# A loop over leftover tokens moves in front of the last group of experts, and TensorE multiplies identities during the routing

## The chip, the cores and the metric

The kernel runs on one core of a Trainium2 chip. The time is the device time of one execution in microseconds (us), the median of several runs. TensorE (PE in the profile) multiplies; VectorE (DVE), ScalarE (ACT) and GpSimd (POOL) do elementwise work; SyncE (SP) issues most DMAs, in the order in which its program has them. Weight loads of TensorE are listed as PEld. Each engine runs its own program in order and waits for the others through semaphores.

## What is computed

One decoder layer on 512 tokens of width 1024, in float32. A state-space mixer and a convolution mixer are added to the residual stream h; then comes a mixture of experts; then a gate with per-layer embeddings p; then a norm. The change touches the mixture of experts and its surroundings:

```
u = rms_norm(h)
group  = argmax(u @ wg + bg)                    # 4 groups of 8 experts
expert = top 2 of the 8 logits in that group    # 1024 assignments, 32 experts
h += sum over the two: weight * (silu(u @ w_gate[e]) * (u @ w_up[e])) @ w_down[e]
h += (p @ w_ple_proj) * sigmoid(rms_norm(h) @ w_ple_gate)
out = rms_norm(h)
```

An expert's three matrices are 1024 x 512, 1024 x 512 and 512 x 1024 numbers, 6 MB together. All 32 experts are read, 192 MB.

## The kernel before

**Stages.** Up to about 530 us of the profile the mixers run. Then the routing picks two experts for each token (lines 1507 to 1592). The experts follow in seven groups (`GROUPS`, from the table `PLAN` in line 52), and last the gate stage, whose steps are the functions named `e_...`.

**Slots.** Each expert has a fixed number of slots for tokens, 32, 64 or 96, by its rank in popularity. A group is one or two "quads" of 128 slots, and a quad is filled by two or three experts. The last group is a single quad of three experts. For a group, `disp` gathers its tokens: four calls, each 16 multiplications of the normalised tokens (`u2h` in tile uh, `u2l` in tile ul) with one-hot matrices, and one copy by ScalarE into a tile cj. `gu_unit` multiplies cj with the gate and up matrices, in four units per quad; `d_unit` multiplies the hidden values with the down matrix, in two units per quad. A unit of a three-expert quad needs three pages of weights of 1 MB each. `combine` adds a group's output back to h (tile Z), in eight calls; each is four multiplications for a group of two quads and two for the last group, and an addition on VectorE. `back` prepares the matrix for it and is the last reader of a group's one-hot matrix.

**Order of the work.** `units` is the list of such units, and `step` runs one: it issues the weight loads for which there is room (`pump`, line 270), then the unit's multiplications, then the jobs hung on that unit. Tasks such as `disp` and `combine` have an earliest and a latest unit, and `after` (line 341) starts them between units where a running credit allows. Weight pages live in a tile w of 11 buffers, some of which hold other data for a time; a load waits until TensorE has read the page that it overwrites. `p_unit` (line 1327) multiplies the embeddings p with w_ple_proj; there are two, placed just ahead of the last group's units. `split_hi` and `split_lo` turn loaded float32 weights into a high and a low part, on ScalarE and VectorE.

**The loop.** Tokens beyond an expert's slots are handled in a hardware loop, `tc.For_i(0, n_ext)` in line 1704, whose count n_ext is computed on the chip. The loop loads an expert's weights in pieces of 512 KB (line 1772). Before it, `run(NC)` has run all units of all groups; after it the gate stage starts with transposes of h (`e_tr`). At the loop SP waits for every load that it has issued, and all engines wait for each other.

Of the kernel before, what the change touches and what calls it, by code (L numbers as in the profile page):

```python
# [52 lines left out]
GROUPS = []  # L53
# [83 lines left out]
def tile_hybrid(ctx: ExitStack, tc: tile.TileContext, x, p, chan, rowv, rows, cst, w_in, w_ssd, w_conf, w_o,  # L137
                rw, eg, eu, ed, w_pg, w_pp, out, dbg=None):
    nc = Core(tc.nc)
# [6 lines left out]
    def st(shape, dt, tag, bufs=1):  # L146
        return sb.tile(shape, dt, name=tag, tag=tag, bufs=bufs)

    def acc():
        return ps.tile([128, 512], F32, name="acc", tag="acc", bufs=6)  # L150
# [4 lines left out]
    def mm(o, a, b, start, stop):  # L155
        nc.tensor.matmul(o, a, b, start=start, stop=stop)
        if b.dtype == F32:
            nc.pe[0] += max(0.1, 3 * o.shape[-1] / 2370)
# [21 lines left out]
    identr = st([128, 128], F32R, "identr")  # L180
# [4 lines left out]
                            pattern=[[1, 128]], channel_multiplier=-1)  # L185
    negr = st([128, 128], F32R, "negr")
    nc.vector.tensor_copy(negr, negm)

    def junk():
        return st([128, D], BF, "k2", 4)  # L190
# [56 lines left out]
    units = []  # L247
# [8 lines left out]
    def unit(src, mms, cost=0.0, plain=False):  # L256
        srcs = [] if src is None else src if isinstance(src, list) else [src]
        units.append(dict(lds=[load(s, plain) for s in srcs], mms=mms, cost=cost, plain=plain))
        return len(units) - 1

    def job(n, f, *a):
        jobs[n].append((f, a))
# [4 lines left out]
    def task(early, late, cost, f, *a):  # L267
        tasks.append((early, late, cost, f, a))
# [86 lines left out]
    def step():  # L355
        n = state["n"]
        top = state["top"]
        if n < NB:
            while state["split"] <= min(max(n + 2, 2 * n - NB + BT["sp"]), top):
                split()  # L360
        else:
            while state["split"] <= min(top, n + BT["hi"]) and split_hi():
                split_lo()
        pump()
        u = units[n]
        if u["plain"]:
            ws = [ld["t"] for ld in u["lds"]]
            u["mms"](ws)
            free(2 * len(ws))
        elif u["mms"] is not None:  # L370
            u["mms"](u["wh"], u["wl"])
        after(u)

    def run(upto=None):
        while state["n"] < (len(units) if upto is None else upto):
            step()
# [517 lines left out]
    n = 0  # L894
# [147 lines left out]
    def p_mm(c, wh, wl):  # L1042
        pj["s"] = pt = acc()
        cs = slice(c * 128, (c + 1) * 128)
        for k in range(2):
            mm(pt, pj["h"][:, k, cs], wh[:, k, :], k == 0, False)
            mm(pt, pj["h"][:, k, cs], wl[:, k, :], False, False)
            mm(pt, pj["l"][:, k, cs], wh[:, k, :], False, k == 1)

    def p_out(n, c):  # L1050
        if c % 2 == 0:
            pj["o", n, c // 2] = page([128, 2, T], F32, "po")
        nc.scalar.activation(pj["o", n, c // 2][:, c % 2, :], pj.pop("s"), AF.Copy, scale=0.5)
# [43 lines left out]
    def rout_mm(c, n):  # L1097
        t = R.pop(("t", c, n))
        for k in range(4):
            mm(R["pl"][:, c * 36:(c + 1) * 36], t[:, k, :], R["rws"][:, 4 * n + k, :],  # L1100
               n == 0 and c == 0 and k == 0, n == 1 and c == NT - 1 and k == 3)
# [97 lines left out]
    def gu_unit(gi, q, i, kp):  # L1199
        quad = GROUPS[gi][q]  # L1200

        def mms(ws):
            if kp == 0:
                PG[gi, q, i] = acc()
            for kk in range(4):
                k = 4 * kp + kk
                strips(PG[gi, q, i], XT[gi, k // 2][:, k % 2, q * QS:(q + 1) * QS], [w[:, kk, :] for w in ws], quad,
                       k == 0, k == KD - 1)
        return unit([lambda b=m[0]: weights((eg, eu)[i], b)[:, 4 * kp:4 * kp + 4, :] for m in quad], mms, BT["mm"],
                    True)  # L1210

    def d_unit(gi, q, fp):
        quad = GROUPS[gi][q]

        def mms(ws):
            if fp == 0:
                PY[gi, q] = [acc2(), acc2()]
            for f in (2 * fp, 2 * fp + 1):
                for n in range(2):
                    strips(PY[gi, q][n], HT[gi, q][:, f, :], [w[:, f % 2, n * 512:(n + 1) * 512] for w in ws], quad,  # L1220
                           f == 0, f == 3)
        return unit([lambda b=m[0]: weights(ed, b)[:, 2 * fp:2 * fp + 2, :] for m in quad], mms, BT["mm"], True)
# [43 lines left out]
    def disp_mm(gi, kp, pt, a):  # L1266
        w = GW[gi]
        for kk in range(2):
            k = 2 * kp + kk
            for c in range(NT):  # L1270
                mm(pt[:, kk * w:(kk + 1) * w], R[("u2h", "u2l")[a]][:, c, k * 128:(k + 1) * 128],
                   G["oh", gi][:, c, :w], a == 0 and kk == 0 and c == 0, a == 1 and kk == 1 and c == NT - 1)

    def disp_out(gi, kp, pt):
        w = GW[gi]
        t = st([128, 2, w], F32, "cj", 9)
        nc.scalar.copy(t, pt[:, :2 * w].rearrange("p (k s) -> p k s", k=2))  # L1277
        XT[gi, kp] = t

    def disp(gi, kp):  # L1280
        pt = acc()
        for a in range(2):
            disp_mm(gi, kp, pt, a)
        disp_out(gi, kp, pt)
# [42 lines left out]
    def p_unit(n):  # L1327
        def mms(wh, wl):
            for c in range(NT):
                p_mm(c, wh, wl)  # L1330
                p_out(n, c)
        return unit(lambda: w_pp.rearrange("(k p) n -> p k n", p=128)[:, :, n * 512:(n + 1) * 512], mms, 5.5)
# [2 lines left out]
        fill_pe(state["n"], room)  # L1335

    combined = NB + 4
    for gi, g in enumerate(GROUPS):
        last = gi == len(GROUPS) - 1
        first = len(units)  # L1340
        if last:
            for n in range(2):
                p_unit(n)
            job(first - 6, free, -2)
            job(first - 5, p_load)
            job(first - 5, free, -2)
            for k in range(2):
                job(first - 3 + k, p_tr, k)
            job(first - 2, free, 2)
            job(first - 2, free, -8)  # L1350
        for q in range(len(g)):
            for kp in range(2):
                for i in range(2):
                    u = gu_unit(gi, q, i, kp)
            job(u - 1, hid_act, gi, q)
            job(u, hid_mul, gi, q)
            job(u, fill_now, BT["fill"][0])
            job(u, hid_tr, gi, q)
            job(u, fill_now, BT["fill"][1])
            if last:  # L1360
                job(u - 1, free, -2)
            for f in range(2):
                u = d_unit(gi, q, f)
            task(combined, u - 1, 1.4, back, gi, q)
            if last:
                job(u - 1, free, -2)
            for n in range(2):
                job(u, y_hi, gi, q, n)
                job(u, y_lo, gi, q, n)
        if last:  # L1370
            for n in range(2):
                for c in range(NT):
                    job(u, combine, gi, c, n)
            continue
        for n in range(2):
            for c in range(NT):
                task(u + 1, u + 5, 0.23 * 2 * len(g), combine, gi, c, n)
        combined = u + 5
        o = first + (BT["late"][0] if gi == 0 else BT["late"][1])
        for q in range(len(GROUPS[gi + 1])):  # L1380
            job(o, hot, gi + 1, q)
        for kp in range(4):
            task(o + 1, u, 0.115 * 16, disp, gi + 1, kp)
    for i in range(3):
        unit(None, None)
    NC = len(units)
# [121 lines left out]
    rout_tr(NT - 1, 1)  # L1508
    for c in (2, 3):
        rout_mm(c, 1)  # L1510
    if dbg == "h1":
        for c in range(NT):
            nc.sync.dma_start(out[c * 128:(c + 1) * 128, :], h[:, c, :])
        return
# [64 lines left out]
    for c in range(NT):  # L1579
        o = pp[:, c * NEXP:(c + 1) * NEXP]  # L1580
# [113 lines left out]
    for k in range(4):  # L1694
        disp_out(0, k, pts[k])
        if k % 2:
            step()
            step()
    run(NC)

    W32 = [128, NEXP]
    ext, ntot, icnt, eidf, pos, gat = (R[n] for n in ("ext", "ntot", "icnt", "eidf", "pos", "gat"))
# [1 line left out]
    with tc.For_i(0, n_ext):  # L1704
# [43 lines left out]
        for k in range(KD):  # L1748
            pt = acc()
# [33 lines left out]
        for w in (eg, eu):  # L1783
            o = acc()
# [9 lines left out]
        pt = acc()  # L1794
# [30 lines left out]
                nc.vector.tensor_add(hv, hv, po)  # L1825
        nc.vector.tensor_scalar(icnt, icnt, 1.0, None, op0=OP.add)
    banks.remove(bank)
    if dbg == "moe":
        for c in range(NT):
            nc.sync.dma_start(out[c * 128:(c + 1) * 128, :], h[:, c, :])  # L1830
        return
# [77 lines left out]
```

## Time and profile before

| | us |
|---|---|
| median of 3 runs (1109.29 to 1111.02) | 1109.32 |
| the profiled execution | 1109.12 |
| its span, first to last instruction | 1107.4 |
| TensorE busy in the span | 1017.9 (92%) |
| VectorE busy | 562.2 (51%) |
| ScalarE busy | 344.6 (31%) |
| mean share of the 16 DMA engines on SP's queue | 60.1% |

TensorE's share is high throughout, and a mean over the span says little, since the stages have different limits. From about 555 to 1034 us the DMA engines are full; before that and after it they are mostly idle. Rows of a timeline give start and duration in us, the engine, the operation, the tile written and the tiles read, the shape, and the count of instructions merged in the row. A float32 multiplication stands as two records, so 32 records of a unit are its 16 instructions. In brackets stands the idle time before and what ended it.

### The profile page before, as it was taken

How to read it: one execution, taken by the hardware profiler on the slowest of the kernel's cores; microseconds unless marked ns; L12 is line 12 of the kernel's file. 1: busy time of each engine (PE TensorE's matmuls, PEld its weight loads, DVE VectorE, ACT ScalarE, POOL GpSimd, SP SyncE). 2: the span in 40 equal slices, each digit the busy share in tenths (PEclk: the TensorE clock that was granted, in tenths of full speed). 3: DMA queues.
4: the chain of work that ended last, by engine and by line, in shares of the span. 5: the costliest groups of instructions: out<-in, count | busy, mean ns of one | idle time of the engine just before them, and what ended most of it. 6: DMA issues, size and time to landing. Idle time of an engine off the chain costs nothing. (4 is left out here: it accounts for less than half of the span.)

```text
span 1107.4 us, 15682 instructions
## 1 busy us (share of the span) xinstructions
PE 1017.9 (92%) x6262; PEld 675.5 (61%) x6262; DVE 562.2 (51%) x1004; ACT 344.6 (31%) x646; POOL 15.5 (1%) x32
## 2 busy tenths in 40 slices
PE   5999999999979989999799998988979989799876
PEld 5788889877868877788634543433525434344555
DVE  6689998897789955663621302203102012022564
ACT  5433446766442234433411110100100101030353
POOL 1000000000000000000000000000000000000020
PEclk9999999999999999999899999999999999999988
DMA  9323232202224323265199999999999999999401
GB/s 268 99 69 107 77 87 67 77 1 77 68 65 118 86 77 114 77 234 222 39 382 388 392 376 423 420 421 421 421 421 420 421 421 420 418 377 422 178 1 76
DMA packets 95660, 255.97 MB, mean 231 GB/s; under 512 B 4784, under 2 KB 62144, under 8 KB 71008
## 3 DMA queue, kind: packets, MB, share of 16 engines
q1 hardware_dynamic: 94896, 252.73, 60.1%
q0 software_dynamic: 688, 2.22, 0.7%
q8 instruction: 50, 0.82, 0.3%
q14 instruction: 26, 0.21, 0.1%
HBM read 252.83 MB, written 2.10 MB: 230 GB/s over the span
## 5 line engine op out<-in xcount | busy, mean ns | idle before, releaser
L120 PE MATMUL acc<-uh,w 128*128 128x512 f32 x704 | 231.0, 401 | 1.7 <-DVE w L120 1.6
L120 PE MATMUL acc<-w,cj 128*32 128x512 f32 x1664 | 203.4, 608 | 17.6 <-DMA w<-eu 10.7
L120 PE MATMUL acc<-w,uh 128*128 128x256 f32 (+2 forms) x752 | 163.8, 328 | 7.6 <-DVE w L120 7.5
L120 PEld LDWEIGHTS acc<-uh,w 128*128 128x128 f32 x704 | 132.3, 188 | 32.7 <-DVE w L120 2.6
L120 PEld LDWEIGHTS acc<-w,cj 128*32 128x32 f32 x1664 | 56.2, 112 | 143.3 <-issue 105.3
L120 PE MATMUL acc<-w,m 128*32 128x512 f32 (+1 forms) x960 | 126.8, 574 | 13.7 <-DMA w<-ed 8.8
L120 PE MATMUL acc<-ul,w 128*128 128x512 f32 x352 | 137.4, 390 | 0.0
L120 PEld LDWEIGHTS acc<-w,uh 128*128 128x128 f32 x752 | 119.7, 194 | 28.6 <-issue 10.2
L120 DVE SCALAR_TENSOR_TENSOR cj<-glu,chan,cj 128x512 f32<-128x512 f32 x180 | 130.9, 748 | 2.2
L120 DVE TENSOR_TENSOR w<-w 128x1024 fp32r<-128x1024 f32 x86 | 104.8, 1221 | 48.4 <-ACT w L302 48.2
L120 PE MATMUL acc<-w,ul 128*128 128x256 f32 (+2 forms) x488 | 118.3, 309 | 0.0
L302 ACT CAST w<-w 128x1024 fp32r<-128x1024 f32 x86 | 89.6, 1051 | 67.8 <-PE acc L120 54.6
L120 PE MATMUL acc<-w 128*128 128x512 f32 x384 | 102.0, 405 | 3.0 <-ACT w L302 2.4
L120 DVE TENSOR_TENSOR k<-k,acc 128x512 f32<-128x512 f32 x21 | 19.1, 911 | 155.5 <-PE acc L120 155.5
L120 PEld LDWEIGHTS acc<-w,m 128*32 128x32 f32 (+1 forms) x960 | 42.9, 124 | 81.1 <-issue 51.9
L120 DVE TENSOR_TENSOR Z<-Z,acc 128x512 f32<-128x512 f32 x64 | 43.4, 687 | 88.1 <-PE acc L120 88.1
L120 PEld LDWEIGHTS acc<-w 128*128 128x128 f32 x384 | 74.0, 194 | 22.0 <-ACT w L302 2.8
L120 PEld LDWEIGHTS acc<-w,ul 128*128 128x128 f32 x488 | 77.7, 190 | 5.6
L120 PEld LDWEIGHTS acc<-ul,w 128*128 128x128 f32 x352 | 66.2, 188 | 14.9 <-issue 1.7
L1226 ACT ACTIVATE k<-acc 128x512 f32<-128x512 f32 x13 | 7.8, 598 | 165.2 <-PE acc L120 165.2
L120 DVE SCALAR_TENSOR_TENSOR w<-glu,chan,w 128x512 f32<-128x512 f32 x60 | 43.0, 748 | 0.7
L1277 ACT COPY cj<-acc 128x512 f32<-128x512 f32 (+1 forms) x28 | 15.6, 555 | 81.9 <-PE acc L120 81.9
(267 smaller groups left out, 880.7 us busy)
## 6 DMA issues: line engine op xcount, KB each, us to landing
w<-eg SPq DMA_DIRECT2D x64, 1024.0 KB, 14.0
w<-eu SPq DMA_DIRECT2D x64, 1024.0 KB, 14.8
w<-ed SPq DMA_DIRECT2D x64, 1024.0 KB, 14.9
w<-w_in SPq DMA_DIRECT2D x52, 512.0 KB, 5.1
w<-w_ssd_out SPq DMA_DIRECT2D x8, 512.0 KB, 4.8
w<-w_conf_out SPq DMA_DIRECT2D x8, 512.0 KB, 4.3
w<-w_o SPq DMA_DIRECT2D x8, 512.0 KB, 4.7
w<-w_ple_gate SPq DMA_DIRECT2D x8, 512.0 KB, 13.3
```

The lines of the kernel that those rows point to most:

```text
L120: return f(*a, **k)
L302: nc.scalar.copy(u["wh"], u["raw"])
L1226: nc.scalar.activation(t, PG.pop((gi, q, 0)), AF.Silu)
L1277: nc.scalar.copy(t, pt[:, :2 * w].rearrange("p (k s) -> p k s", k=2))
```

## The change

The loop moves from behind the last group to a place ahead of it: units run up to `NL`, which is the end of the two `p_unit`s, then comes the loop, then the last group. The last group's `disp` is no longer a task spread over the group before; it is called four times right behind the loop. The combines of the group before the last get an earlier latest unit, so that all eight are done ahead of the loop. Separately, `warm(21)` puts 21 multiplications of the identity with itself into TensorE's program between the router's multiplications and the first one that counts tokens; nobody reads their result.

```
+    def warm(n, pt=None):
+
+        pt = acc() if pt is None else pt
+        for _ in range(n):
+            nc.tensor.matmul(pt, identr, identr[:, None, :].to_broadcast([128, pt.shape[1] // 128, 128]), start=True,
+                             stop=True)
...
         if last:
             for n in range(2):
                 p_unit(n)
+            NL = len(units)
...
-                task(u + 1, u + 5, 0.23 * 2 * len(g), combine, gi, c, n)
+                task(u + 1, u + (5 if gi < len(GROUPS) - 2 else 2), 0.23 * 2 * len(g), combine, gi, c, n)
...
         for kp in range(4):
-            task(o + 1, u, 0.115 * 16, disp, gi + 1, kp)
+            if gi < len(GROUPS) - 2:
+                task(o + 1, u, 0.115 * 16, disp, gi + 1, kp)
...
     for c in (2, 3):
         rout_mm(c, 1)
+    warm(21)
...
-    run(NC)
+    run(NL)
...
     banks.remove(bank)
+    for kp in range(4):
+        disp(len(GROUPS) - 1, kp)
+    run(NC)
```

On TensorE, in the routing, the difference is one row. The tile glu holds the router's weights, k the transposed tokens, identr the identity, and dtx the matrix that counts the tokens of each expert.

```order
 L120 MATMUL acc_3902<-glu,k_4161 128x36 x4
 L120 MATMUL acc_3902<-glu,k_4168 128x36 x4
+L120 MATMUL acc<-identr 128x512 x21
 L120 LDWEIGHTS dtx
 L120 MATMUL acc<-dtx 128x32
```

The 21 stand between the last row of the router and the first row of the count.

On SP, at the last group's weights, before (numbers are buffers; the loads named are the second and third page of the first eu unit, the next eg page, and the last load ahead of the loop at the end):

```order
L282 DMA w_7389<-eu 128x2048
L282 ISA
L282 DMA w_7480<-eu 128x2048
L282 ISA
L282 DMA w_7482<-eg 128x2048
...
L282 DMA w_7713<-w_ple_gate 128x2x512
L1703 TENSOR_LOAD cd_4503
```

The same place on SP after the change, where cd holds the loop's count:

```order
L289 DMA w_7335<-eu 128x2048
L1714 TENSOR_LOAD cd_4525
L1714 ISA x2
L1715 COMPARE_AND_BRANCH
L1715 UNCONDITIONAL_BRANCH x2
...
L1715 UNCONDITIONAL_BRANCH
L289 ISA
L289 DMA w_7950<-eu 128x2048
L289 ISA
L289 DMA w_7952<-eg 128x2048
```

The loop now stands behind the fifth of the last group's 18 pages; the other 13 and all eight loads of w_ple_gate are behind it.

On TensorE, ahead of the last group, before (w alone is a `p_unit`, w with cj is a `gu_unit`, the four rows with glu are one `combine`):

```order
L120 MATMUL acc<-w 128x512 x24
L120 MATMUL acc<-w,cj 32x512 x32
L120 MATMUL acc<-ct,glu 128x512
L120 MATMUL acc<-btok,glu 128x512
L120 MATMUL acc<-k_7356,glu 128x512
L120 MATMUL acc<-bt,glu 128x512
```

And after, where w with uh or ul is half a `disp`:

```order
L120 MATMUL acc<-k_7302,glu 128x512
L120 MATMUL acc<-bt,glu 128x512
L1714 TENSOR_LOAD cd
L1715 COMPARE_AND_BRANCH
L1715 UNCONDITIONAL_BRANCH x2
...
L1715 UNCONDITIONAL_BRANCH
L120 MATMUL acc<-w,uh 128x128 x8
L120 MATMUL acc<-w,ul 128x128 x8
...
L120 MATMUL acc<-w,cj 32x512 x48
```

Seven combines now stand between the second `p_unit` and the loop, and the four `disp` between the loop and the first unit of the last group; before, two units of the last group came directly behind the second `p_unit`.

## Rows read from the trace of the kernel before

**Rows 1.** DMA issues by line, from the page: count, size, us to landing.
```profile
w<-eg SPq DMA_DIRECT2D x64, 1024.0 KB, 14.0
```

**Rows 2.** Busy time by stretch: PE, PEld, DVE, ACT, POOL, then PEclk, DMA share, GB/s.
```profile
800.00:850.00 50.00, 42.67 (x300) 15.68 (x292) 9.44 (x16) 3.15 (x5) 0.00 (x0) 0.97 1.01 420
992.00:994.00 2.00, 2.00 (x14) 0.96 (x16) 0.00 (x0) 1.08 (x2) 0.00 (x0) 1.00 0.44 184
```

**Rows 3.** Timeline of TensorE, 993 to 1031 us.
```profile
993.14 7.07 PE L120 MATMUL acc<-w,cj 128*32 128x512 f32 x64
...
1001.17 0.40 PE L120 MATMUL acc<-ct,glu 128*128 128x512 f32 x1
...
1005.00 3.64 PE L120 MATMUL acc<-w,cj 128*32 128x512 f32 x32
...
1027.10 3.62 PE L120 MATMUL acc<-w,m 128*32 128x512 f32 x26 [1.52 <-DMA w<-ed]
```

**Rows 4.** Timeline of SP, the last group's loads.
```profile
980.43 0.90 SPq L282 DMA_DIRECT2D w<-eu  x2
986.86 0.33 SPq L282 DMA_DIRECT2D w<-eu  x1
993.24 0.91 SPq L282 DMA_DIRECT2D w<-eg  x2
996.81 0.33 SPq L282 DMA_DIRECT2D w<-eg  x1
```

**Rows 5.** DMA issues of 993.0 to 993.5 us, then of 996 to 997 us.
```profile
w<-eg SPq DMA_DIRECT2D x1, 1024.0 KB, 5.0
...
w<-eg SPq DMA_DIRECT2D x1, 1024.0 KB, 7.8
```

**Rows 6.** Timeline of VectorE, two combines' additions.
```profile
1002.31 0.69 DVE L120 TENSOR_TENSOR Z<-Z,acc 128x512 f32<-128x512 f32 x1 [0.24 <-PE acc L120]
1003.24 0.69 DVE L120 TENSOR_TENSOR Z<-Z,acc 128x512 f32<-128x512 f32 x1 [0.24 <-PE acc L120]
```

**Rows 7.** Timeline of all engines at the loop, 1034 to 1041 us.
```profile
1034.74 0.39 PE L120 MATMUL acc<-btok,glu 128*128 128x512 f32 x1
1036.92 1.22 DVE L120 TENSOR_TENSOR w<-w 128x1024 fp32r<-128x1024 f32 x1
...
1038.65 3.00 PE L120 MATMUL acc<-ident,Z 128*128 128x128 f32 x16 [3.53 <-DVEq L1704]
...
1040.17 0.75 DVE L120 SCALAR_TENSOR_TENSOR ul<-acc,chan,uh 128x512 fp32r<-128x512 f32 x1 [2.03 <-ACT uh L218]
```

**Rows 8.** Timeline of SP, behind the loop.
```profile
1038.50 0.38 SPq L282 DMA_DIRECT2D w<-w_ple_gate  x1
```

**Rows 9.** Timeline of TensorE, the starts of two of the last group's gathers.
```profile
945.34 1.11 PE L120 MATMUL acc<-w,uh 128*128 128x128 f32 x8
947.18 1.06 PE L120 MATMUL acc<-w,uh 128*128 128x128 f32 x8
```

**Rows 10.** Busy time by stretch, behind the loop.
```profile
1040.00:1042.00 2.00, 2.00 (x10) 1.90 (x9) 1.75 (x2) 2.00 (x4) 0.00 (x0) 0.50 0.93 327
```

**Rows 11.** Timeline of TensorE, the routing and the first gather.
```profile
530.49 1.98 PE L120 MATMUL acc<-glu,k 128*128 128x36 f32 x16 [0.35 <-ACT k L1094]
538.07 0.45 PE L120 MATMUL acc<-dtx 128*128 128x32 bf16 x10 [5.60 <-DVE dtx L120]
539.45 6.48 PE L120 MATMUL acc<-w,uh 128*128 128x256 f32 x32 [0.93 <-DVE w L120]
545.76 3.93 PE L120 MATMUL acc<-w,ul 128*128 128x256 f32 x32
```

**Rows 12.** Timeline of VectorE, the low parts of the tokens.
```profile
540.23 5.38 DVE L120 SCALAR_TENSOR_TENSOR ul<-cj,rst,uh 128x512 fp32r<-128x512 f32 x8
```

**Rows 13.** Busy time by stretch, in the routing.
```profile
532.00:534.00 2.00, 0.47 (x5) 0.35 (x4) 1.66 (x9) 1.51 (x3) 0.00 (x0) 1.00 0.31 131
540.00:542.00 2.00, 2.00 (x10) 1.91 (x10) 2.00 (x4) 0.00 (x0) 0.00 (x0) 0.50 0.01 4
```

More of the change, by code (lines that the diff above doesn't have):

```diff
@@ L1337, in tile_hybrid @@
     combined = NB + 4
+    NL = None
     for gi, g in enumerate(GROUPS):
```

## The prediction

> **What bounds the kernel now.** I read the table by stretch first. From 560 to 1034 us the DMA engines are full: 420 GB/s at a share of 1.01, while TensorE is busy for 42.67 of 50 us [rows 2]. In this stretch a microsecond in which the DMA engines stand still is a microsecond lost, and one in which TensorE stands still mostly costs nothing. A page of 1 MB (1.05 million bytes) takes 1.05 / 0.42 = 2.5 us of it. Next I read where the stretch ends. TensorE's timeline shows the last down unit of the last group starting at 1027.10 on a wait for ed, the last expert page [rows 3]; so the last page's landing sets when the experts end. Then the list of DMA issues: eg was loaded 64 times in pieces of 1024 KB, two for each of 32 experts, and no piece of 512 KB is in the list (eu and ed read alike) [rows 1]. So the loop ran zero times, and all it costs is its waits. Those stand in the timeline at the loop: TensorE's last combine starts its last multiplication at 1034.74, VectorE ends its last piece of work at 1036.92 + 1.22 = 1038.14, and only then SP issues again (1038.50) and TensorE goes on (1038.65, after 3.53 us idle) [rows 7, 8]. From the last arrival the barrier takes 0.36 us to SP and 0.51 us to TensorE. Last I read the routing, where the DMA engines stand still because every page is full (share 0.01) and TensorE runs at a granted clock of 0.50, the 1.2 GHz level [rows 13].
>
> **The multiplications in the routing.** TensorE ends the router at 530.49 + 1.98 = 532.47 and idles 5.60 us until the count at 538.07 [rows 11]. The granted clock is still 1.00 at 532 to 534 and 0.50 at 540 to 542 [rows 13]. The nearest row to the 21 new ones, which are 512 columns each, is a combine: four multiplications of 512 columns in 0.93 us [rows 6], so 0.233 each and 4.9 for 21. They end at 537.4, before the count's operand is there; at half clock they would take 9.8 us and end at 542.2. I take the first, since the clock is 1.00 where they start. What they buy: the 32 gathers with uh take 6.48 us and the 32 with ul 3.93 us at the higher clock [rows 11], so 2.55 us are to be had at most. But the ul gathers read what VectorE writes in eight pieces that end at 540.23 + 5.38 = 545.61 [rows 12]. With the uh half done at about 544, the first four ul gathers still wait for the last piece, and the other 28 run from 545.6, in 28/32 of 3.93 = 3.4 us, to 549.1 instead of 545.76 + 3.93 = 549.69. That is **-0.6 us**. The DMA engines start again with the first pages freed behind this, so the 0.6 is carried through the full stretch. Bounds: -1.2, if the count also gets faster by its 0.45 us of work, and +4.1, if the 21 end at 542.2 and hold up the count by 542.2 - 538.07.
>
> **The loop in the middle.** Times here are on the axis of the trace of before. In before the first unit of the last group follows the second p unit at 993.14 [rows 3]. Now seven combines of 0.93 us [rows 6] come first: 6.5 us, to 999.65. The last one starts at 998.7; from a combine's first multiplication (1001.17) to the end of its addition (1002.31 + 0.69 = 1003.00) it is 1.83 us [rows 3, 6], so VectorE is the last to arrive, at 1000.55. With the barrier's 0.36 and 0.51 SP issues again at 1000.9 and TensorE goes on at 1001.05. Queued behind the wait on SP are 13 of the last group's 18 pages and all eight loads of w_ple_gate; in before the first of these 13 went out at 986.86 and the next two from 993.24 on [rows 4]. Of POOL's queue only the gain of the final norm stands behind it, which is needed much later.
>
> Ahead of the loop only three eg pages and two eu pages are loaded, and the room is then taken or blocked, so the DMA engines run dry. At 1000.9 three loads go out at once, into buffers that are free by then, and the fourth page, the last eg, waits until TensorE has read the first unit's pages. TensorE first does four gathers of 947.18 - 945.34 = 1.84 us [rows 9], 7.4 us, to 1008.4. ScalarE's copies of them run beside the next gather. Then the first unit: in before, eg went out 996.81 - 993.14 = 3.67 us after that unit's start [rows 3, 4], so now at 1012.1. The three pages issued at 1000.9 are moved by about 1010, so the engines run dry a second time.
>
> The shift can be counted from two landings. A page issued into a nearly idle queue at 993.24 landed after 5.0 us [rows 4, 5], which makes 1017.1 for the fourth page; in before it landed at 996.81 + 7.8 = 1004.6. That is +12.5 us. Or from issue to the end: before, twelve pages from an idle start at 993.24 to the last wait's end at 1027.10 took 33.9 us [rows 3, 4]; now ten pages from 1012.1 take two pages less, 28.9, to 1041.0. That is +13.9 us. I take the mean, **+13.2 us**, as both start from rows of the same place. Behind the fourth page the pages are freed early enough to keep the engines full (the second and third unit free six more by about 1021). What was removed from the group before, two gathers at 945 to 949 [rows 9] among them, was hidden under full DMA engines and gives back nothing.
>
> The Trainium skill ("DMA: Bandwidth & Descriptors", section "Anatomy of one DMA — SWDGE (gpsimd) path") gives a DMA 2.0 us and its bytes at 436 GB/s, for DMAs issued by GpSimd. By that the fourth page would land 0.6 us earlier than by the 5.0 us of the row, an estimate, and the sum would be 10.5; no row has a page alone in the queue, so the trace neither bears it out nor denies it.
>
> **The end without the loop.** After the last combine TensorE can go on at once with the transposes. In before it began them at 1038.65, and the first low part of h (tile ul) was written at 1040.17 on VectorE, which waited 2.03 us for ScalarE and so for the transposes [rows 7]. Without the barrier that piece starts as soon as VectorE has ended its own work at 1038.14, so 2.0 us earlier, and no more than that although TensorE's gap is 3.5 us: VectorE is late next. TensorE then still waits piecewise for VectorE, and in before the granted clock was 0.50 at 1040 to 1042 after such a gap [rows 10]. I charge 0.5 us for a lower clock and take **-1.5 us**. Bounds: 0, if the lower clock falls on the dense part, and -3.5, if all of TensorE's gap comes back.
>
> The Trainium skill ("TensorE: Matmul & The Clock Gate", section "Part 4: PE-mode transpose") says that transposes do not count as TensorE being busy for its clock. Rows 10 agree in so far as the clock fell to 0.50 while the transposes from 1038.65 ran, but the gap ahead of them would explain it as well. By that rule the clock falls here with or without the loop, the end term is 0, and the sum is 12.6.
>
> **The sum.** -0.6 + 13.2 - 1.5 = +11.1 us. The profiled execution took 1109.12 us, 1.7 more than its span of 1107.4, and lies 0.2 under the median of 1109.32. So 1109.12 + 11.1 = **1120.2 us**, about 1% slower.
>
> **Rivals.**
> First, the pages carry it. The last group's five loaded pages and the three that go out at once could bridge the barrier, if its pages do not set the end; then only -0.6 and -1.5, or -3.5 at best, are left: 1107.0, or 1105.0, faster. For it: TensorE has 7.4 us of gathers and two units to do before it needs a new page. Against it: it decides by whether the last page's landing has some 13 us to spare, and TensorE waited for just that page at 1027.10 [rows 3]; already in before the DMA share fell to 0.44 at 992 to 994 [rows 2]. Chance 0.08.
> Second, the group before ends earlier. Its units are rid of the gathers, so pages would be freed and fetched earlier, and TensorE would be at the loop up to 5 us sooner. That makes 1120.2 - 5 = 1115.2. Against it: a share of 1.01 leaves no room to fetch earlier. Chance 0.10.
> Third, the change doesn't do what it says in the routing: the 21 run at the lower clock and hold up the count. Instead of -0.6 it is +4.1: 1124.9. Chance 0.05.
>
> **How the numbers follow.** The forecast has 0.77; its own range, from 12.5 - 1.2 - 3.5 = +7.8 to 13.9 - 0.6 + 0 = +13.3, is 1116.9 to 1122.4. With the second and third rival the range is 1114.5 to 1125. What a measurement can tell from no change is 0.2%, 2.2 us, so faster begins at 1107.1. The first rival lies about there: faster 0.06, within 0.2% 0.03, slower 0.91.
>
> **What would show it.** If I am right, the DMA row of the changed kernel falls to nothing for about 10 us around 992 to 1002 and again shortly before 1014; the last ed wait ends 12 to 14 us later than 1027; the transposes follow the last combine with no wait on the loop; the granted clock stays at 1.00 through the routing, and the uh gathers take about 4 us. I am wrong if the DMA engines stay busy around the loop, if SP issues pages while TensorE still does the combines, or if the uh gathers are not faster.

## The result, and the profile after

| | before | after |
|---|---|---|
| median (6 runs each, side by side) | 1111.19 us | 1130.07 us |
| lowest to highest | 1109.29 to 1113.35 | 1120.68 to 1131.89 |
| the profiled execution, its span | 1109.12, 1107.4 | 1130.83, 1129.0 |
| mean granted clock in the profiled span | 0.975 | 0.970 |

The ratio over all rounds is 1.0157, with an interval of 1.0134 to 1.0180 (the medians alone give 1.0170): slower by 1.6%, where 1% was forecast. The six times of after are not spread evenly. Two, 1120.68 and 1122.22, had a mean granted clock of 0.978; four, 1129.73 to 1131.89, had 0.967 to 0.973. The forecast of 1120.2 is the lower group; the median, and the profile, fall in the upper one. The experiments fall in the same two groups, called here the lower and the upper level. Two runs of the experiments, at mean clocks of 0.55 and 0.71, are left out below.

First, TensorE's timeline in after, from the last combine ahead of the loop to the gate stage; it answers to [rows 3, 7, 9]. The rows w with uh or ul are half a gather each, w with cj is a gate or up unit, w with m a down unit.

```profile
999.57 0.39 PE L120 MATMUL acc<-bt,glu 128*128 128x512 f32 x1
1002.10 1.71 PE L120 MATMUL acc<-w,uh 128*128 128x128 f32 x8 [2.15 <-issue]
1003.61 1.91 PE L120 MATMUL acc<-w,ul 128*128 128x128 f32 x8
...
1013.85 1.91 PE L120 MATMUL acc<-w,ul 128*128 128x128 f32 x8
1015.68 9.79 PE L120 MATMUL acc<-w,cj 128*32 128x512 f32 x70
...
1049.86 5.32 PE L120 MATMUL acc<-w,m 128*32 128x512 f32 x26 [1.50 <-DMA w<-ed]
...
1059.24 0.39 PE L120 MATMUL acc<-btok,glu 128*128 128x512 f32 x1
1059.47 1.91 PE L120 MATMUL acc<-ident,Z 128*128 128x128 f32 x16
```

The order is the one forecast: seven combines, a stop of 2.15 us at the loop, four gathers, the first unit. VectorE ends the last combine's addition in between, at 999.99 + 0.69 = 1000.68:

```profile
999.99 0.69 DVE L120 TENSOR_TENSOR Z<-Z,acc 128x512 f32<-128x512 f32 x1 [0.23 <-PE acc L120]
```

But half a gather takes 1.7 us, where in before a whole one took 1.84 [rows 9]. The table by stretch says why (busy PE, PEld, DVE, ACT, POOL, then PEclk, DMA share, GB/s; stretches overlap):

```profile
992.00:1002.00 10.00, 7.96 (x35) 6.16 (x33) 4.81 (x7) 1.20 (x2) 0.00 (x0) 1.00 0.01 3
1002.00:1014.00 12.00, 11.90 (x57) 11.90 (x58) 0.00 (x0) 1.12 (x3) 0.53 (x1) 0.52 0.85 308
1004.00:1018.00 14.00, 14.00 (x68) 12.16 (x71) 0.00 (x0) 1.49 (x4) 0.00 (x0) 0.50 0.61 232
1014.00:1022.00 8.00, 8.00 (x53) 3.28 (x56) 0.00 (x0) 0.37 (x1) 0.00 (x0) 0.66 0.00 0
1018.00:1020.00 2.00, 2.00 (x16) 0.52 (x12) 0.00 (x0) 0.00 (x0) 0.00 (x0) 0.63 0.00 0
1020.00:1022.00 2.00, 2.00 (x24) 0.60 (x20) 0.00 (x0) 0.00 (x0) 0.00 (x0) 1.00 0.00 0
1022.00:1050.00 28.00, 20.72 (x150) 6.08 (x142) 1.65 (x5) 1.76 (x3) 0.00 (x0) 1.00 1.00 405
1058.00:1066.00 8.00, 5.96 (x33) 4.38 (x32) 8.00 (x11) 5.26 (x7) 0.00 (x0) 1.00 0.09 33
```

The granted clock is 0.50, the 1.2 GHz level, from 1004 to 1018, all through the gathers and into the first unit; TensorE is busy for 14.00 of these 14 us. The DMA engines stand dry twice, at 992 to 1002 (share 0.01) and at 1014 to 1022 (0.00). The second dry spell ends when SP can issue the page that the first unit frees. SP's timeline, and the list of DMA issues from 1021 to 1021.5 (its last column is us to landing):

```profile
1001.30 0.35 SPq L289 DMA_DIRECT2D w<-eu  x1
...
1021.23 0.33 SPq L289 DMA_DIRECT2D w<-eg  x1
...
w<-eg SPq DMA_DIRECT2D x1, 1024.0 KB, 4.8
```

That page went out at 1021.23, where 1012.1 was forecast. Nearly the whole miss stands in that one row.

The routing in after answers to [rows 11, 13]; timeline of TensorE, then two stretches.

```profile
530.87 1.98 PE L120 MATMUL acc<-glu,k 128*128 128x36 f32 x16 [0.35 <-ACT k L1101]
532.68 5.04 PE L120 MATMUL acc<-identr 128*128 128x512 f32 x21
538.45 0.40 PE L120 MATMUL acc<-dtx 128*128 128x32 bf16 x10 [0.73 <-DVE dtx L120]
539.78 6.18 PE L120 MATMUL acc<-w,uh 128*128 128x256 f32 x32 [0.93 <-DVE w L120]
...
549.66 2.78 PE L120 MATMUL acc<-w,cj 128*32 128x512 f32 x24
```

```profile
540.00:542.00 2.00, 2.00 (x12) 1.61 (x12) 2.00 (x5) 0.00 (x0) 0.00 (x0) 0.91 0.01 4
542.00:544.00 2.00, 2.00 (x11) 2.00 (x11) 2.00 (x4) 0.00 (x0) 0.00 (x0) 0.50 0.03 8
```

The 21 run at the higher clock and hold up nothing; the low clock then comes at 542 to 544 instead of 540 to 542, so the uh gathers take 6.18 us instead of 6.48.

### The profile page after: what moved, and what is told of

Its sections match the earlier page's. It is cut to its first block, busy times and chain, and to the rows that moved or that the text cites. A ratio compares the mean times of both kernels' runs of the same rounds, so it can differ in the third digit from the quotient of the medians.

```text
span 1129.0 us, 15733 instructions
## 1 busy us (share of the span) xinstructions
PE 1035.6 (92%) x6283; PEld 681.7 (60%) x6283; DVE 562.0 (50%) x1004; ACT 345.0 (31%) x646; POOL 15.3 (1%) x32
## 5 line engine op out<-in xcount | busy, mean ns | idle before, releaser
L120 PE MATMUL acc<-w,m 128*32 128x512 f32 (+1 forms) x960 | 134.1, 602 | 21.9 <-DMA w<-ed 16.5
L120 PE MATMUL acc<-w,ul 128*128 128x256 f32 (+2 forms) x488 | 121.4, 318 | 1.0 <-DVE ul L120 1.0
L120 PEld LDWEIGHTS acc<-w,ul 128*128 128x128 f32 x488 | 81.1, 199 | 7.2 <-DVE ul L120 1.7
L120 DVE COPY gt<-acc 32x1 f32<-32x1 f32 x52 | 8.0, 154 | 80.3 <-PE acc L120 79.8
L120 DVE SCALAR_TENSOR_TENSOR bt<-acc,gt,k 128x512 fp32r<-128x512 f32 x12 | 9.0, 750 | 69.1 <-ACT k L1317 68.6
## 6 DMA issues: line engine op xcount, KB each, us to landing
w<-w_ple_gate SPq DMA_DIRECT2D x8, 512.0 KB, 13.6
```

Source lines behind the costliest of these rows:

```text
L120: return f(*a, **k)
```

## The experiments

The theories after this reading. A: the place in the order (seven combines and four gathers ahead of the unit that frees pages) costs some 10 us, and the low clock behind the loop the other 9. B: the multiplications in the routing set the rhythm of the clock, and so the upper level. C: the drain at the loop, where SP waits for every load, costs it all. Each kernel was run five rounds beside the kernel before; ratios are to before in the same rounds.

**The loop's move alone.** After, without the 21 multiplications.

```
-    warm(21)
```

> The changed kernel without the 21 multiplications in the routing: the moved loop alone. Theory A (TensorE's clock behind the loop makes the part that the forecast missed): the times of the changed kernel come back, 1120 to 1122 us in executions with a mean granted clock near 0.978 and 1129 to 1132 us in those near 0.970, since the routing gave only 0.3 us; in the profile the four gathers behind the loop take 7.4 us at a granted clock of 1.00 or 13.7 us at 0.50. Theory B (the multiplications in the routing shift the clock's rhythm later on and cause the slow level): one level, about 1121 us, and the gathers always at 1.00.

Measured: median 1130.44, ratio 1.0156 (1.0127 to 1.0185), one run at 1122.02 and five at 1129.39 to 1131.92. Both levels are there without the 21; B falls. The run at 1122.02 had a mean clock of 0.970, no higher than some runs of the upper level, so the mean clock alone does not tell the levels apart.

**The multiplications alone.** Before, with them (and the definition of `warm`).

```
+    warm(21)
```

> The kernel before with the 21 multiplications in the routing and nothing else. The trace of the changed kernel has the granted clock at 1.00 until 541 us and at 0.50 from 542 to 544, so the fall is put off and not taken away: I expect -0.3 us, a ratio of 0.999 to 1.001, no difference that can be measured. By the forecast's term it is -0.6 us. If they hold up the count it is +4 us.

Measured: ratio 1.0005 (0.9992 to 1.0019). No difference can be told; -0.3 lies within it.

**After without the loop, order kept.**

```
-    n_ext = nc.values_load(ntot, min_val=0, max_val=T * 2 // SL + NEXP)
-    with tc.For_i(0, n_ext):
...
```

> The changed kernel with the loop taken out (it runs zero times on these tokens; tokens beyond the slots are left out), its order of work kept: seven combines and four gathers ahead of the last group's first unit. Theory A, first half (the order costs, not the drain): the page that the first unit frees goes out at 999.8 + 7.4 + 3.7 = 1011 us instead of 997, the last page lands 12 to 13 us later than before, the gate stage gains 2.9 us, in all +9 to +10 us, 1120 us, and one level, as TensorE never idles there and its clock stays at 1.00. Theory C (SP's wait for its loads and the barrier cost all of it): without them nothing is lost, and it takes 3 us less than before, 1108 us.

Measured: median 1120.79 (1117.36 to 1123.32), ratio 1.0078 (1.0056 to 1.0099), one level. TensorE's timeline:

```profile
997.79 0.39 PE L120 MATMUL acc<-bt,glu 128*128 128x512 f32 x1
998.02 1.00 PE L120 MATMUL acc<-w,uh 128*128 128x128 f32 x8
...
1004.22 1.05 PE L120 MATMUL acc<-w,ul 128*128 128x128 f32 x8
1005.21 7.92 PE L120 MATMUL acc<-w,cj 128*32 128x512 f32 x70
```

With no stop the four gathers take 1005.21 - 998.02 = 7.2 us, as priced, and by the medians the order makes the kernel 9.9 us slower (1120.79 against 1110.86 in these rounds), although the loop's waits are gone from it altogether. C falls as the cause of it all.

**Before without the loop.** The same edit on before, at the end of the experts.

```
     run(NC)
...
-    with tc.For_i(0, n_ext):
...
```

> The kernel before with the loop taken out (it runs zero times on these tokens; tokens beyond the slots are left out). It prices the loop at its old place. From the last combine's last multiplication to the end of the span it was 72.7 us before and 69.8 us in the changed kernel: I expect -2.9 us, a ratio of 0.997 to 0.998. By the forecast's term it is -1.5 us.

Measured: median 1109.83, ratio 0.9993 (0.9976 to 1.0009). TensorE's last combine:

```profile
1035.13 0.39 PE L120 MATMUL acc<-btok,glu 128*128 128x512 f32 x1
```

The miss is one of size: in its trace the way from there to the end of the span, 1106.2, is 1.6 us shorter than in before (71.1 against 72.7), not 2.9; the forecast had 1.5. In the times that is too little to tell. It also bounds what any place for the loop can bring: with no loop at all the gain is about 1 us by the medians, and at most 2.7 by the interval.

**The gathers ahead of the loop.** The last group's gathers again in the group before; for room, the loop's body is cut to one instruction.

```
-            if gi < len(GROUPS) - 2:
-                task(o + 1, u, 0.115 * 16, disp, gi + 1, kp)
+            task(o + 1, u, 0.115 * 16, disp, gi + 1, kp)
...
-    for kp in range(4):
-        disp(len(GROUPS) - 1, kp)
```

> The changed kernel with the loop's body cut to one instruction (it runs zero times here in either form) and the last group's four gathers issued again inside the group before, so that the first unit, which frees the pages, stands directly behind the loop. Left out: the work of the loop's body, of which nothing runs here. Theory A (order and clock): the page freed by the first unit is issued near 1006 instead of 1021, the gathers cost nothing ahead (the group before waits for its pages, whose last unit stood at 977.6 with the gathers and at 977.8 without), the level with the low clock behind the loop goes or shrinks to 2 us: 1115 to 1119. If the drain and the barrier at the loop cost the time: no better than the upper level of the changed kernel, 1121.

Measured: median 1120.35 (1117.94 to 1121.86), ratio 1.0095 (1.0077 to 1.0113). No run lies in the upper level, but 1120.35 lies above the 1115 to 1119 expected. TensorE's timeline behind the loop:

```profile
1004.41 4.49 PE L120 MATMUL acc<-w,cj 128*32 128x512 f32 x38 [1.47 <-DVEq L1714]
...
1013.15 1.05 PE L120 MATMUL acc<-w,cj 128*32 128x512 f32 x4 [0.19 <-DMA w<-eg]
1016.02 1.04 PE L120 MATMUL acc<-w,cj 128*32 128x512 f32 x2 [1.82 <-DMA w<-eg]
```

The first unit does follow the loop, and its page goes out at 1008.08. But the next units now wait for the pages that SP could issue only behind the loop. Theory A had no room for this: with the gathers out of the way, the drain is what is late.

**Three pages ahead of the loop.** The order of after; eu3, eg4 and eg5 (the pages that in after go out right behind the loop) are issued ahead of it.

```
     run(NL)
+    free(6)
+    pump()
+    free(-6)
```

> The changed kernel with the three pages that wait for nothing behind the loop (eu3, eg4, eg5) issued ahead of the loop, so that they land while it drains. Theory A: they were not late, as the first page missed is the one that the first unit frees at 1021; no change, the same two levels of 1121 and 1130. If the drain of the transfers is the price (theory C): about 7.5 us earlier, the share of the dry spell that these three pages fill.

Measured: median 1128.65 (1120.00 to 1133.44), ratio 1.0167 (1.0134 to 1.0201), against 1.0157 for after: no gain that can be told. By stretch:

```profile
994.00:1000.00 6.00, 6.00 (x28) 4.87 (x27) 3.77 (x6) 0.60 (x1) 0.00 (x0) 1.00 0.83 309
1006.00:1020.00 14.00, 14.00 (x72) 9.46 (x74) 0.00 (x0) 1.12 (x3) 0.00 (x0) 0.54 0.01 3
```

The first dry spell is filled (share 0.83), and the second grows by as much: 14 us at 0.01, until the first unit frees its page.

**Both ahead.** The two edits above in one kernel, with the loop's body cut to one instruction as for the gathers ahead.

```
     run(NL)
+    free(6)
+    pump()
+    free(-6)
...
-            if gi < len(GROUPS) - 2:
-                task(o + 1, u, 0.115 * 16, disp, gi + 1, kp)
+            task(o + 1, u, 0.115 * 16, disp, gi + 1, kp)
```

> The two edits tried apart so far, together: the last group's gathers inside the group before, and the three pages that wait for nothing (eu3, eg4, eg5) issued ahead of the loop; the loop's body cut to one instruction (left out: its work, of which nothing runs here). By the dry time (the time that the transfers stand still between 980 and 1030 is the time lost): alone, the gathers ahead left 13.8 us of it and the pages ahead 21.9 (22.1 in the changed kernel), since each left the other gap open. Together the drain is filled by the three pages, and what stays is from their landing near 1001 to the first unit's end near 1008, with 2 to 3 us ahead of the loop: 10 to 11 us dry, 3 us less than with the gathers ahead alone, 1116 to 1118.5. If the two edits work apart from one another (pages ahead brought nothing alone): 1120 as with the gathers ahead. If it is the drain alone: 1113.

Measured: median 1114.52, ratio 1.0030 (1.0016 to 1.0045). Together the two edits bring more than either alone (1120.35 and 1128.65), and more than the estimate: 7.5 us dry (table below) in place of the 10 to 11 expected. What the pages add to the gathers ahead is a fair comparison, as both kernels have the short body. What the gathers add to the pages ahead is not: that kernel has the whole body, and pages ahead with a short body were not run.

**Sixteen multiplications behind the loop.**

```
+    warm(16)
     for kp in range(4):
         disp(len(GROUPS) - 1, kp)
```

> The changed kernel with 16 multiplications of 512 columns by the identity right behind the loop, ahead of the four gathers: work added on the path. If the clock behind the loop is what splits the times in two levels (theory A): the granted clock is back at 1.00 before the gathers begin, these take 7.2 instead of 13.65 us, and the two levels (1121 and 1130) move toward one another, to 1124 to 1128. If the clock is no cause: every run is later by the 3.7 to 6.8 us of the added work, 1125 and 1135 to 1137.

Measured: median 1128.49, all within 1126.83 to 1128.58, ratio 1.0170 (1.0152 to 1.0189). TensorE's timeline:

```profile
1003.13 3.92 PE L120 MATMUL acc<-identr 128*128 128x512 f32 x16 [2.15 <-issue]
1006.89 1.00 PE L120 MATMUL acc<-w,uh 128*128 128x128 f32 x8
```

The stop is the same 2.15 us, and in the profile the clock did not fall: it is 1.00 from 998 to 1024. The times have drawn together, with a median just above the 1124 to 1128 expected: the 3.7 us of added work are paid, and the spread between the two levels is gone. That no run pays for slow gathers fits the five times, but only one of them was profiled.

**A small loop.** The order of after, the loop's body cut to one instruction.

```
     with tc.For_i(0, n_ext):
-        bank = [st([128, 512], F32, "k2", 4), 0]
...
         nc.vector.tensor_scalar(icnt, icnt, 1.0, None, op0=OP.add)
```

> The changed kernel with the loop's body cut to one instruction, order as in the changed kernel. TensorE came back 1.42 us behind the last addition there, and 0.51 us at the end loop of the kernel before. If the way past a long body costs that (its instructions are fetched anew): TensorE stands still for 1.2 instead of 2.15 us, total 0.9 us earlier, and the low level of the clock comes less often, so the median falls toward 1120. If not: two levels as before, 1121 and 1130, most runs in the upper one. Left out: the work of the loop's body, of which nothing runs here.

Measured: median 1121.81, ratio 1.0135 (1.0105 to 1.0164); four runs at 1119.72 to 1121.99, two at 1127.87 and 1129.36. The profiled one, 1119.72, shows the lower level from inside. TensorE:

```profile
1000.66 1.11 PE L120 MATMUL acc<-w,uh 128*128 128x128 f32 x8 [1.46 <-DVEq L1715]
...
1007.96 7.92 PE L120 MATMUL acc<-w,cj 128*32 128x512 f32 x70
...
1040.40 3.62 PE L120 MATMUL acc<-w,m 128*32 128x512 f32 x26 [1.45 <-DMA w<-ed]
```

SP:

```profile
1011.62 0.33 SPq L289 DMA_DIRECT2D w<-eg  x1
```

Gathers in 7.3 us, the page out at 1011.62, the last wait for ed over at 1040.40. The prediction had 7.4, 1012.1 and 1041.0. The stop is 1.46 us (1.47 with the gathers ahead, which has the short body too); the long body costs 0.7 us more to get past. Whether the upper level comes less often with the short body cannot be told from these times: the interval overlaps that of after (1.0134 to 1.0180).

**Five multiplications ahead of the loop.**

```
+    warm(5)
     n_ext = nc.values_load(ntot, min_val=0, max_val=T * 2 // SL + NEXP)
```

> The changed kernel, whole loop body and order, with five multiplications of 512 columns by the identity (1.2 us) behind the last combine, ahead of the loop. VectorE adds up to 1.1 us beyond TensorE's last multiplication there, so the barrier comes no later; TensorE's stop shrinks from 2.15 to 1.0 to 1.4 us. If that stop is what lets the clock fall: the upper level goes, 1120 to 1122 in all or nearly all runs, gathers of 0.9 us a half. If the clock falls for another reason (the turn of the gathers' shape, the program's fetch): two levels, 1121 and 1130, as in the changed kernel.

Measured: median 1131.03, one run at 1122.56 and five at 1128.37 to 1132.15; ratio 1.0159 (1.0131 to 1.0188). TensorE:

```profile
1000.50 1.31 PE L120 MATMUL acc<-identr 128*128 128x512 f32 x5
1003.91 1.11 PE L120 MATMUL acc<-w,uh 128*128 128x128 f32 x8 [2.10 <-issue]
1004.85 1.73 PE L120 MATMUL acc<-w,ul 128*128 128x128 f32 x8
```

VectorE, the last addition:

```profile
1000.70 0.69 DVE L120 TENSOR_TENSOR Z<-Z,acc 128x512 f32<-128x512 f32 x1 [0.23 <-PE acc L120]
```

The edit failed: the stop only moved, and is 2.10 us still. Here VectorE was done at 1001.39, ahead of TensorE's last multiplication (1001.81), so the stop was no wait for VectorE: with the whole body TensorE needs some 2.1 us from its own arrival. It tells nothing on whether the stop is the cause of the upper level.

**A stop without a loop.** After without the loop, and in its place a copy on VectorE and one multiplication that waits for it.

```
+    stop = st([128, 512], F32R, "k2", 4)
+    nc.vector.tensor_copy(stop, h[:, NT - 1, 512:])
+    nc.tensor.matmul(acc(), identr, stop, start=True, stop=True)
```

> The changed kernel without the loop (left out: the work beyond the slots, of which there is none here), with a stop of TensorE set where the loop stood: VectorE copies the last strip of the sum behind its last addition (0.7 us), and one multiplication, whose product nobody reads, waits for that copy; ahead of the gathers, TensorE stands still for some 2.1 us, as at the loop, but no transfer is drained. If the stop lets the clock fall and the fall is the upper level: of the 1120.8 without the stop, runs in two groups, near 1122 to 1123 and near 1129 to 1132, gathers of 1.7 us a half in the slower ones. If the fall belongs to the loop itself (barrier, drain, program fetch): one group near 1122.5, later by the stop alone.

Measured: median 1121.71, ratio 1.0105 (1.0080 to 1.0130), five runs at 1119.22 to 1123.53 and one at 1127.90. TensorE:

```profile
1002.36 0.50 PE L120 MATMUL acc<-k,identr 128*128 128x512 f32 x1 [1.24 <-DVE k L120]
1002.70 1.00 PE L120 MATMUL acc<-w,uh 128*128 128x128 f32 x8
```

In the profile the stop came out at 1.24 us, not 2.1, and the clock held at 1.00; not the test that was meant. So it was made longer:

```
+    for n in range(4):
+        nc.vector.tensor_copy(stop, h[:, NT - 1, 512:])
```

> The kernel without the loop and with a stop, the stop made longer: four copies of VectorE instead of one ahead of the multiplication that waits, for the one copy left TensorE standing 1.24 us where 2.1 was meant (left out as there: the work beyond the slots, of which there is none here). From 1.24 and 0.4 a copy: a stop of 2.3 to 2.5 us, just over the 2.15 at the loop. If a stop of that length lets the clock fall, with no drain and no barrier: most runs near 1130 to 1132, gathers of 1.7 us a half in them, few near 1122 to 1123. If the fall belongs to the loop itself: all near 1122 to 1123.5, later than with the short stop by some 1.1 us.

Measured: median 1132.26 (1129.75 to 1135.72), ratio 1.0186 (1.0169 to 1.0203): every run in the upper level. TensorE, then a stretch:

```profile
999.01 0.39 PE L120 MATMUL acc<-bt,glu 128*128 128x512 f32 x1
1002.03 0.80 PE L120 MATMUL acc<-k,identr 128*128 128x512 f32 x1 [2.63 <-DVE k L120]
1002.62 1.80 PE L120 MATMUL acc<-w,uh 128*128 128x128 f32 x8
...
1014.46 1.91 PE L120 MATMUL acc<-w,ul 128*128 128x128 f32 x8
```

```profile
1004.00:1006.00 2.00, 2.00 (x11) 2.00 (x11) 0.00 (x0) 0.00 (x0) 0.00 (x0) 0.50 0.00 0
```

Here is no loop, no barrier and no drain, only TensorE standing still for 2.63 us in front of the gathers, and the gathers take the 1.7 us a half of after. Without the stop the same kernel had no run above 1123.32, with it none below 1129.75; the stop and its one multiplication are themselves 3.2 of the 11.5 us between the medians. This is what shows the cause of the upper level: a stop in front of the gathers, through the clock.

**One measure for all.** The time that the DMA engines stand dry, 50 x (1 - share) for the stretch 980 to 1030, against the start of TensorE's last down unit behind its wait for ed. The stretch in before, in after and with both ahead:

```profile
980.00:1030.00 50.00, 46.61 (x293) 23.79 (x289) 11.01 (x17) 8.90 (x15) 0.00 (x0) 0.97 0.98 395
980.00:1030.00 50.00, 47.25 (x253) 32.36 (x246) 9.37 (x12) 9.02 (x17) 0.53 (x1) 0.83 0.56 219
980.00:1030.00 50.00, 42.09 (x247) 21.32 (x249) 8.41 (x15) 6.70 (x12) 0.54 (x1) 0.90 0.85 337
```

| kernel | share | dry us | last ed wait over | later than before |
|---|---|---|---|---|
| before | 0.98 | 1.0 | 1027.10 | |
| both ahead | 0.85 | 7.5 | 1033.53 | 6.4 |
| after, no loop | 0.77 | 11.5 | 1038.05 | 11.0 |
| small loop | 0.73 | 13.5 | 1040.40 | 13.3 |
| gathers ahead | 0.73 | 13.5 | 1042.25 | 15.2 |
| sixteen behind the loop | 0.63 | 18.5 | 1046.39 | 19.3 |
| after | 0.56 | 22.0 | 1049.86 | 22.8 |
| long stop, no loop | 0.55 | 22.5 | 1050.43 | 23.3 |

A microsecond of dry time is about a microsecond at the end, to within some 3 us. It holds so for the profiles not in the table: the loop's move alone, the pages ahead and the five ahead of the loop have 22.0 us dry and are 21.7 to 22.9 later, the short stop has 13.0 and 15.4, and before with the multiplications alone or without the loop has 1.5 and 1.0 and is 0.6 earlier and 0.4 later. Part of the scatter is that the profiles do not reach this stretch at the same time: the group before ends its last wait for ed at 974.91 with both ahead, at 977.57 in before and at 980.77 with the gathers ahead. Counted from there, these two are 9.1 and 12.0 later than before. The measure says where the time lies; what makes the engines run dry is shown by the experiments.

## Why the prediction went wrong, point by point

**What bounds it: right.** The full DMA engines carry the stretch, and the last page sets when the experts end; the table above is that sentence in numbers.

**The way to the loop: right for SP, 1 us short for TensorE.** The last combine starts its last multiplication at 999.57, SP issues at 1001.30 (forecast 1000.9). TensorE goes on at 1002.10, forecast 1001.05: the barrier's 0.51 us from before is 1.42 behind VectorE's last addition here. The forecast counted from the last arrival; by the kernel with five multiplications ahead of the loop, TensorE needs 2.1 us from its own. In before that would have been hidden, as VectorE ended its work 3.0 us behind TensorE's last multiplication.

**The step that failed: "TensorE first does four gathers of 947.18 - 945.34 = 1.84 us [rows 9], 7.4 us, to 1008.4", and "3.67 us" for the first unit behind them.** Both rows come from a place where the clock was 1.00 and TensorE had not stopped. Behind the loop they took 1015.68 - 1002.10 = 13.6 us and 1021.23 - 1015.68 = 5.55 us. With the barrier's 1.05 that is 6.2 + 1.9 + 1.05 = 9.1 us, the page at 1021.23 instead of 1012.1. No run of after in its lower level was profiled, but the small loop's profile, which lies there, has 7.3 us and 1011.62, and in it the step holds. So the mechanism was right and the gathers' price was that of the wrong clock in four runs of six. A row that points to it was there: the prediction itself read that the clock fell to 0.50 behind the 3.53 us stop at the end loop [rows 10] and charged 0.5 us for it there, but charged nothing behind the stop in the middle. That stop it had at 1.4 us, from 999.65 to 1001.05, and the profiles with stops of 1.24 to 1.47 us kept the clock at 1.00; it came out at 2.15. As far as these profiles show, the 1 us too little for the barrier and the missing 8 us for the clock are one miss.

**From the page to the end: right.** From the page's issue to the last wait's end it was 1049.86 - 1021.23 = 28.6 us, forecast 28.9. By the Trainium skill ("DMA: Bandwidth & Descriptors", section "Anatomy of one DMA — SWDGE (gpsimd) path"), whose figures are for DMAs that GpSimd issues, a page alone in the queue takes 4.4 us, an estimate; after has such a page, issued by SP at 1021.23 in a dry stretch, and it landed after 4.8, nearer to the 5.0 of [rows 5]. Not in any term: the last down unit fell in a stretch of low clock and took 5.32 us instead of 3.62 [rows 3], +1.7.

**The end: right in sign, too small.** From the last combine's last multiplication to the end of the span it is 1129.0 - 1059.24 = 69.8 us, against 1107.4 - 1034.74 = 72.7: -2.9 instead of -1.5, within its bounds. The transposes follow with no wait. Taking the loop out of before gave 1.6 us in its trace, close to the forecast; where the other 1.3 us in after come from stays open. The rule of the Trainium skill ("TensorE: Matmul & The Clock Gate", section "Part 4: PE-mode transpose") by which this term would be 0 did not show here: the transposes ran at 1059.47 for 1.91 us, and the clock stayed at 1.00 from 1058 to 1066. (With both edits ahead it did fall, to 0.50 at 1048 to 1050, 5 us behind the end of the transposes; so a later fall there is not excluded.)

**The routing: right in sign, smaller.** The way from the router's end to the first unit is 549.66 - 532.85 = 16.8 us, where before had 549.6 - 532.47 = 17.1: -0.3 instead of -0.6, and the runs with the multiplications alone cannot tell it from nothing (1.0005). That the clock would stay at 1.00 there and the uh gathers take 4 us was wrong; the fall was put off, not prevented.

**The sum.** On the axis of the trace the last wait's end was to shift by -0.6 + 13.2 = 12.6 us and shifted by 22.8, 10.2 too little. Add 1.7 for the last unit and take off 1.4 at the end: 10.5, the difference of the spans (1129.0 against 1107.4 + 11.1).

**The rivals.** The pages do not carry the loop. The group before did not end earlier: its p units stand at 981.35 and 987.85, against 981.12 and 987.59 in before. The 21 hold up nothing. The range had no case for a low clock behind the loop, and that is where the time came out.

**Order and drain.** The forecast counted one chain, the page that the first unit frees, and that is the one that was late. What it did not see is that the drain stands ready behind it: the gathers ahead alone or the pages ahead alone leave the kernel 10 to 20 us slower, both together 3.7 us (1114.52 against 1110.85; the short body of the loop, part of two of these kernels, has its share). None of these kernels beats before, and without any loop only about 1 us could be had, so no better place for the loop was looked for.

## What to carry to other kernels

Where full DMA engines set the pace, price a moved step by the time for which they then run dry, and look for every page that can be late, not the first alone: closing one gap may only widen the next. A duration read at the higher clock need not be the price behind a stop of TensorE; where a stop elsewhere in the trace is followed by the lower clock, take a second case with durations read at that clock, and a chance for it. A step that many others wait for should not stand right behind a stop.

## What the runs showed of the hardware

TensorE's clock did not rise although TensorE was busy without a gap: in after it was 0.50, the 1.2 GHz level, from 1004 to 1018 (14.00 of 14.00 us busy), on gathers of 128 columns with a weight load for each and on the start of the first unit; it was 0.63 at 1018 to 1020 and 1.00 from 1020, in the 512-column multiplications of that unit. The same gathers ran at 1.00 at 945 to 949 of before and in after without the loop, where no stop stood ahead of them.

In the profiles, stops of 2.03 to 2.63 us at this place were followed by a clock of 0.50 six times of seven; the seventh is the kernel with sixteen multiplications behind the stop. After the three stops of 1.24 to 1.47 us the clock held at 1.00. The times of the kernels with the gathers behind this place go the same way. Above 1126 us lie none of six runs without a stop, one of six with a stop of 1.24 us, two of six with 1.46, 19 of 24 with 2.10 to 2.15 (after, its loop alone, the pages ahead, the five ahead of the loop) and five of five with 2.63, where each length is that of one profiled run. What decides from run to run stays open.

The way past a loop that runs zero times depended on the length of its body. Counted from TensorE's own last multiplication ahead of the last group it was 2.10 to 2.15 us with the whole body, in five kernels, and 1.46 and 1.47 with one instruction in it, in two. At the end of before TensorE went on 0.51 us behind VectorE, but 3.53 behind its own last multiplication; so the 2.1 us had passed there already, which fits, but was not tried by itself.
